# A diffusion-transformer layer on one core: four small moves of work between engines, steps and banks

## The chip, the core and the metric

The kernel runs on one NeuronCore of a Trainium2 chip. The metric is the time of one execution on the device in microseconds, and of several executions the median. A core has a matrix engine (TensorE, in the profile PE, its weight loads PEld), an engine for elementwise work and reductions (VectorE, DVE), one for activations (ScalarE, ACT), a general one (GpSimd, POOL) and one that issues DMAs (SyncE, SP). Each works through its own instructions strictly in program order and waits on semaphores for the others.

## What is computed

One layer of a transformer with two kinds of heads, over a sequence of 2048 rows of width 1024, beside a context of 256 rows:

```
h = modulate(rmsnorm(x), shift1, scale1);  hc likewise from the context
rq, rk, rv, rg, aq, ak, av = split(h @ w_in)      # context: rk, rv, ak, av only
ret = bidirectional chunked retention (4 heads of 128, chunk 128) on rope(rq), rope(rk), rv
ret = groupnorm(ret) * gn_g * silu(rg)
att = softmax attention, 8 query heads over 2 key heads of 64, keys = context + sequence
x   = x + g1 * (concat(ret, att) @ w_out)
h2  = modulate(rmsnorm(x), shift2, scale2)
x   = x + g2 * (relu(h2 @ w_ff1)**2 @ w_ff2)      # 1024 -> 4096 -> 1024
out = rmsnorm(x) * final_norm_g
```

Shifts, scales and gates come from a product of a conditioning vector with w_mod. All inputs are 32-bit floats; query and key heads are normalized ahead of the rotation (rope).

## The kernel before

Products are made of halves: an operand is split into a high half and a low remainder (16-bit, scaled by a power of two that depends on the operand's largest value), and three matmuls (high by high, high by low, low by high) add up in one PSUM bank. That is why maxima of the weights are needed: `greatest_of` loads a piece of a later weight (512 KB, L916) and VectorE takes its greatest magnitude into `wmx` (L919). 32 pieces are treated so.

**Input projection (to about 600 us).** The work of TensorE is a list of units, each one tile of 128 rows by one block of columns of w_in (24 matmuls, L1192 to L1194). The order of everything else is written out by hand: `do(s, part, fn)` files a piece of work under step s, and after each unit `run_step(s)` issues what is filed for that step, in the order of `PARTS`:

```
PARTS = ("hi", "evac", "turned", "low", "vec", "pool", "root", "aux", "turn", "load", "store")
```

"hi" holds the high halves of weights (ScalarE, L536) and keys, "evac" the copies of finished units out of PSUM (ScalarE, L699), "turned" the copies of turned retention heads (ScalarE, L740, tile zs), "low" the low halves (VectorE, L543), "vec" the rotation (VectorE, L635 to L650, which makes ys and kn), "aux" the maxima and rows of the modulation (VectorE, L919 and L380), "turn" the transposes by TensorE into one of two PSUM banks of the pool psT (tile psx: retention heads L711, attention keys L837), "load" and "store" the DMAs on SP's queue. Loads of w_in (L517, tile wst), of w_mod (L369, wmo) and of pieces for maxima (L916, wm) share one ring of six buffers under the tag "wst" (L301). A buffer goes to the next load in the order in which the loads are issued, and that load starts when the buffer's last user is done.

For an attention key tile whose unit is at step s (L815 to L842): split high at s+4 (ScalarE) and low at s+5 (VectorE, L832), `turn_k` at s+6 (TensorE, L837), and at s+7 the copy of the two turned blocks, 128 x 256, into `ks` (L842). Eighteen tiles have such a copy. For a retention query or key tile `turn` is at s+4 and `turned` at s+5.

**Attention, retention and output (to about 1460 us).** Here the order is a table of events: `on(k, phase, fn)`, with 36 events for each of the 16 tiles of rows, from the last tile (c = 15) to the first. A group of events holds score products (L210, L211, exponentials on ScalarE L216, high half L220, low half on GpSimd L227 or VectorE L229, products with values L242 to L245). A tile's retention output is copied out at event k+10, its statistics made at k+12 and k+13 (VectorE), the root and the row mr (GpSimd, L1689) in a chain behind, then four norms (ScalarE, L1695, one for each head) and the gating (GpSimd, L1699). The transposes of the gated rows (TensorE, L1815) follow at k+24 and the output product after that (L1833 to L1835). Tile t gets its residual sum (VectorE, L1840), norm (GpSimd, L1860), transposes (L1865), modulation (VectorE, L1870), shift (GpSimd, L1875) and the store of h2. For t = 0, the last, these four steps are not events but entries of the list `rest`, of which two are issued in each early step of the next stage.

**Feed-forward (from about 1462 us).** Up and down projections in seven Strassen products each. A job of the up-projection is 12 matmuls (L2071 to L2073) into one PSUM bank of the ring `ff["ps"]`; VectorE adds the result to its partners (L2083). The weights are summed by GpSimd, converted high by ScalarE (L2047) and low by VectorE (L2053). `Ring` (L1976) hands out slots in turn. It has four banks from the start, gets two more when `open_late` runs, and the last two when `rest` is empty (L2421 to L2425): these are the two banks that held the last tile's transposed rows. `extend` puts new slots ahead of the old ones, so that they are the next to be used; a tile in a bank starts when the bank's former reader is done.

Of the kernel before, what the change touches and what calls it, by code (L numbers as in the profile page):

```python
# [16 lines left out]
AF = mybir.ActivationFunctionType  # L17
ALU = mybir.AluOpType
AX = mybir.AxisListType
PSUM = bass.MemoryType.PSUM  # L20
DRAM = bass.MemoryType.DRAM

P = 128
# [33 lines left out]
def layer_kernel(ctx: ExitStack, tc: tile.TileContext, a: dict, out: bass.AP):  # L57
    nc = tc.nc
# [211 lines left out]
    with ExitStack() as st, tc.manual_schedule():  # L270
# [36 lines left out]
        def do(s, part, fn, *args):  # L307
            steps.setdefault((s, part), []).append((fn, args))
# [380 lines left out]
        def post(s, g, col, kind, i, x):  # L689
# [59 lines left out]
            elif col == C_RG:  # L749

                def gated():
                    nc.gpsimd.tensor_tensor(new_y(), x["x"], gnb, op=ALU.mult)

                def greatest():
                    nc.vector.tensor_reduce(
                        wmx[:, 72 + i : 73 + i], x["y"], axis=AX.X, op=ALU.max, apply_absolute_value=True
                    )

                do(s + 1, "evac", evac, AF.Silu)
                do(s + 2, "pool", gated)  # L760
                do(s + 3, "vec", greatest)
                do(s + 3, "store", lambda: nc.sync.dma_start(rg_d[i], x["y"]))
            elif col == C_AQ:
                att_tables(s, x, i)
                do(s + 1, "evac", evac)
                head_norm(s + 1, x, 8, "q", scale)
                rope(
                    s + 2,
                    x,
                    lambda: heads(new_y(), 8),  # L770
                    lambda: heads(x["x"], 8),
                    lambda: x["tb"][:, 0, 0],
                    lambda: x["tb"][:, 0, 1],
                    8,
                    HD,
                    lambda: bc(x["r"].unsqueeze(2), [P, 8, HD]),
                )
                do(s + 4, "turn", turn)

                def high():  # L780
                    x["z"] = op.tile([P, 2, 4, P], F16, name="qhl", tag="zs")
                    nc.scalar.activation(x["z"][:, 0], x["pt"], AF.Copy)

                def low():
                    nc.vector.tensor_tensor(x["z"][:, 1], x["pt"], x["z"][:, 0], op=ALU.subtract)

                do(s + 5, "turned", high)
                do(s + 5, "vec", low)
                do(s + 6, "store", lambda: nc.sync.dma_start(aq_d[i], x["z"]))
            else:  # L790
                do(s + 1, "evac", evac, AF.Copy, 256)
                src = lambda: x["x"][:, 128:256].rearrange("p (g d) -> p g d", g=2)
                do(s + 2, "store", lambda: nc.sync.dma_start(av_d[:, :, row], src()))
                head_norm(s + 1, x, 2, "k", scale)

                def new_k():
                    x["kn"] = op.tile([P, 2, 2, HD], F32, name="kn", tag="kn", bufs=4)
                    return x["kn"][:, :, 0]

                r = lambda: bc(x["r"].unsqueeze(2), [P, 2, HD])  # L800
                if kind == "c":

                    def plain():
                        w = bc(g2[:, 1, 0].unsqueeze(1), [P, 2, HD])
                        nc.gpsimd.tensor_tensor(new_k(), heads(x["x"][:, :128], 2), w, op=ALU.mult)

                    do(s + 2, "pool", plain)
                    do(
                        s + 3,
                        "vec",  # L810
                        lambda: nc.vector.tensor_tensor(x["kn"][:, :, 0], x["kn"][:, :, 0], r(), op=ALU.mult),
                    )
                else:
                    att_tables(s, x, i)
                    rope(  # L815
                        s + 2,
                        x,
                        new_k,
                        lambda: heads(x["x"][:, :128], 2),
                        lambda: x["tb"][:, 1, 0],  # L820
                        lambda: x["tb"][:, 1, 1],
                        2,
                        HD,
                        r,
                    )

                def high():
                    x["kh"] = op.tile([P, 2, HD], F16, name="kh", tag="kh")
                    nc.scalar.activation(x["kh"], x["kn"][:, :, 0], AF.Copy)

                def low():
                    nc.vector.tensor_tensor(x["kn"][:, :, 1], x["kn"][:, :, 0], x["kh"], op=ALU.subtract)  # L832

                def turn_k():
                    x["pt"] = psT.tile([P, 4, P], F32, name="psx", tag="psx")
                    for g in range(2):
                        nc.tensor.transpose(x["pt"][:, g], x["kn"][:, g].rearrange("p a b -> p (a b)"), ident)  # L837

                do(s + 4, "hi", high)
                do(s + 5, "low", low)  # L840
                do(s + 6, "turn", turn_k)
                do(s + 7, "vec", lambda: nc.vector.tensor_copy(ks[:, :, row * P : (row + 1) * P], x["pt"][:, :2]))  # L842

        def value_parts(s):

# [64 lines left out]
        def greatest_of(i, s):  # L910

            x = {}

            def load():
                x["w"] = raw("wm").rearrange("p a b -> p (a b)")
                nc.sync.dma_start(x["w"], piece_of(i))  # L916

            def reduce():
                nc.vector.tensor_reduce(wmx[:, i : i + 1], x["w"], axis=AX.X, op=ALU.max, apply_absolute_value=True)  # L919

            do(s - 1, "load", load)
            do(s, "aux", reduce)

        def magnitude_of(i, s):
# [609 lines left out]
    def on(k, phase, fn, *args):  # L1534
        events.setdefault((k, phase), []).append((fn, args))
# [74 lines left out]
    def retention(k0):  # L1610
# [110 lines left out]
        for n in range(NT):  # L1721
            c, k = NT - 1 - n, R0 + RF * n
            on(k - 8, "dma", take, c, "qt", "kt")
            on(k - 4, "late", decay, c, "qf", tf)
            on(k - 3, "late", decay, c, "qb", tb)
            on(k - 11, "dma", take, c + NC, *(("rk", "rv") if c > 0 else ("rv",)))
            on(k - 2, "dma", take, c, "f")
            on(k + 2, "pe", score, c, (0, 1, 2, 3))
            on(k + 4, "late", mask, c)
            for h in range(4):  # L1730
                on(k + 6 + h, "pe", head, c, h)
            if c > 0:
                on(k - 8 if n else k - 2, "late", weigh, 1, c + NC)
                on(k + 5, "pe", product, c + NC, 0, (0, 1, 2, 3))
                on(k + 8, "late", update, 1, c + NC, ("b", c), ("b", c - 1), "sb", (0, 1))
                on(k + 9, "late", update, 1, c + NC, ("b", c), ("b", c - 1), "sb", (2, 3))
            on(k + 10, "late", ocopy, c)
            on(k + 12, "dma", take, c, "gate")
            on(k + 12, "late", stats, c, (0, 1))
            on(k + 13, "late", stats, c, (2, 3))  # L1740
            on(k + 13, "late", root, c)
            for h in range(4):
                on(k + (16 + h // 2 * 2 if c > 0 else 15 + h // 2), "late", norm, c, h)
            on(k + (20 if c > 0 else 17), "late", gated, c)


    rest = []
# [56 lines left out]
    def output_tile(t, k, last):  # L1804
# [95 lines left out]
            return made  # L1900
        if t == 1:
            for q in range(2):
                on(k + 79 + q, "pe", transpose_x, q)
                on(k + 80 + q, "early", modulate, q)
                on(k + 81 + q, "late", shift_, q)
                on(k + 82 + q, "dma", store_h, q)
            return made
        on(k + 68, "pe", transpose_x, 0)
        on(k + 70, "early", modulate, 0)
# [66 lines left out]
    class Ring:  # L1976
# [4 lines left out]
            for slot in slots:  # L1981
                self.extend(*slot)

        def extend(self, pool, tag, n):
            at = self.n % max(len(self.slots), 1)
            self.slots = [(pool, tag, n)] * n + self.slots[at:] + self.slots[:at]
            self.n = 0

        def tile(self, shape, dtype, name):
# [418 lines left out]
    with tc.manual_schedule():  # L2408
        for k in range(min(events)[0], max(events)[0] + 1):
            for phase in PHASES:  # L2410
                run(k, phase)
                if phase in ("maximum", "low", "late"):
                    link()
        assert not events and not chain
        up_jobs()
        down_jobs()
        k = min(events)[0]
        while events:
            for phase in FPHASES:
                run(k, phase)  # L2420
                if phase == "pe" and rest and k > 1:  # L2421
                    rest_steps(2)
                    if not rest:
                        banks.close()
                        ff["ps"].extend(pool(late_ff, "fp3", space=PSUM), "p", 2)  # L2425
            k += 1


# [58 lines left out]
```

## Time and profile before

| | |
|---|---|
| time, median of 3 runs | 2643.18 us (2641.77 to 2645.54) |
| the profiled execution | 2639.86 us, of which the span is 2638.0 us |
| mean granted clock of TensorE | 0.997 |
| ScalarE, VectorE, GpSimd busy | 1504.4, 2045.0, 1761.0 us |
| moved by DMA | 481.84 MB, mean 183 GB/s |

The durations below are from the profiled execution. A row of the timeline gives the start in the span, the busy time, engine, line, operation, output and inputs with their shapes, and in brackets how long the engine had been idle before it and what ended that. The rows of waits sum such idle time by the instruction that waited and the one that released it. A row of windows gives, for a stretch of the span, the busy time of each engine with the number of its instructions, then TensorE's granted clock (1.00 is full speed), the mean busy share of the DMA engines, and GB/s.

### The profile page before, as it was taken

What the parts mean: (1) busy time and instruction counts of PE and PEld (TensorE: products, weight loads), DVE (VectorE), ACT (ScalarE), POOL (GpSimd) and SP (SyncE); (2) the same over time, 40 slices, a digit from 0 to 9 for tenths busy, and PEclk for the clock granted to TensorE, in tenths of its full rate; (3) what the DMA queues carried; (4) which work ended last, traced back from release to release, by engine and by line L of the source; (5) the groups of instructions that cost most, each with busy time, mean ns of one, the idle gap of its engine ahead of it and who ended that gap; (6) DMA issues with size and microseconds to landing.
All of it is one profiled execution on the core that took longest, in us unless ns stands there. A gap on an engine that the chain in (4) does not pass through costs nothing.

```text
span 2638.0 us, 45431 instructions
## 1 busy us (share of the span) xinstructions
PE 2595.5 (98%) x16617; PEld 1449.8 (55%) x16617; DVE 2045.0 (78%) x3098; ACT 1504.4 (57%) x2544; POOL 1761.0 (67%) x1451
## 2 busy tenths in 40 slices
PE   8999999999999999999999999999999999999998
PEld 5885555546666666666666444444444444444443
DVE  5788898667888888888887697899886665656686
ACT  3865343427877787888788576666665322222243
POOL 3644566546676678798887685777662566666686
PEclk9999999999999999999999999999999999999999
DMA  7776999737122132333332855777684748475453
GB/s 232 274 254 222 306 328 318 263 113 228 45 71 59 57 112 74 101 85 117 97 86 72 295 156 153 239 226 231 216 295 144 277 170 303 162 285 183 153 190 114
DMA packets 332903, 481.84 MB, mean 183 GB/s; under 512 B 90228, under 2 KB 200068, under 8 KB 328200
## 3 DMA queue, kind: packets, MB, share of 16 engines
q1 hardware_dynamic: 332664, 478.94, 54.9%
q8 instruction: 130, 2.13, 0.3%
q14 instruction: 93, 0.76, 0.1%
q10 hardware_dynamic: 16, 0.01, 0.0%
HBM read 321.89 MB, written 156.38 MB: 181 GB/s over the span
## 4 chain that ended last, share of the span: by engine, by line
PE 69%; ACT 3%; POOL 2%; DVE 1%; DMA 1%; issue 1%; DVEq 0%; POOLq 0%; ACTq 0%; SPq 0%
PE pd L2300 7%; PE pd L2298 7%; PE pd L2299 7%; PE pu L2071 7%; PE pu L2073 7%; PE pu L2072 7%; PE st L210 4%; PE o L245 4%; PE st L211 4%; PE mp L177 3%; PE o L243 2%; PE bank L1835 2%; PE bank L1833 2%; PE bank L1834 2%; ACT p L216 1%; ACT phi L220 1%
## 5 line engine op out<-in xcount | busy, mean ns | idle before, releaser
L190 DVE TENSOR_REDUCE nm<-mp 128x1 f32<-128x512 f32 x558 | 377.6, 685 | 88.3 <-PE mp L177 82.9
L216 ACT ACTIVATE p<-st 128x512 f32<-128x512 f32 x576 | 341.6, 600 | 153.7 <-PE st L211 148.0
L227 POOL TENSOR_TENSOR plo<-p,phi 128x1024 f16<-128x1024 f32 x160 | 348.8, 2186 | 83.2 <-ACT phi L220 83.1
L2071 PE MATMUL pu<-hf,w1f 128*128 128x512 f16 x896 | 339.6, 379 | 3.7 <-DVE u L1870 2.9
L2073 PE MATMUL pu<-hf,w1f 128*128 128x512 f16 x896 | 339.6, 379 | 0.4 <-DVE w1f L2053 0.4
L2298 PE MATMUL pd<-w,uf 128*128 128x512 f16 x896 | 339.6, 379 | 0.0
L2299 PE MATMUL pd<-w,uf 128*128 128x512 f16 x896 | 339.6, 379 | 0.0
L2300 PE MATMUL pd<-w,uf 128*128 128x512 f16 x896 | 339.6, 379 | 0.0
L2072 PE MATMUL pu<-hf,w1f 128*128 128x512 f16 x896 | 339.6, 379 | 0.0
L2318 POOL TENSOR_TENSOR y<-y,d 128x512 f32<-128x512 f32 x128 | 210.7, 1649 | 143.1 <-ACT uf L2287 98.6
L220 ACT ACTIVATE phi<-p 128x1024 f16<-128x1024 f32 x288 | 305.2, 1060 | 0.0
L229 DVE TENSOR_TENSOR plo<-p,phi 128x512 f16<-128x512 f32 x256 | 236.0, 923 | 21.8 <-ACT phi L220 9.4
L243 PE MATMUL o<-wv,plo 128*128 128x65 f16 x2304 | 230.1, 193 | 0.7 <-POOL plo L227 0.5
L245 PE MATMUL o<-wv,phi 128*128 128x129 f16 x2176 | 228.4, 220 | 0.0
L210 PE MATMUL st<-qr,ks 128*128 128x512 f16 x576 | 218.0, 379 | 10.3 <-ACT p L216 7.9
L243 PEld LDWEIGHTS <-plo 128*128 128x128 f16 x2304 | 205.1, 98 | 29.8 <-POOL plo L227 1.7
L2310 DVE SCALAR_TENSOR_TENSOR y<-pd,scy,y 128x512 f32<-128x512 f32 x160 | 116.9, 747 | 131.9 <-PE pd L2300 130.6
L211 PE MATMUL st<-qr,ks 128*128 128x512 f16 x576 | 218.2, 379 | 0.0
L2083 DVE TENSOR_TENSOR r<-pu,r 128x512 f32<-128x512 f32 x224 | 149.9, 684 | 83.9 <-PE pu L2073 59.9
L1192 PE MATMUL pso<-wf,h_l 128*128 128x512 f16 (+1 forms) x576 | 208.9, 363 | 0.0
L1193 PE MATMUL pso<-wf,h_l 128*128 128x512 f16 (+1 forms) x576 | 208.7, 362 | 0.0
L1194 PE MATMUL pso<-wf,h_l 128*128 128x512 f16 (+1 forms) x576 | 208.6, 362 | 0.0
(394 smaller groups left out, 6109.2 us busy)
## 6 DMA issues: line engine op xcount, KB each, us to landing
wm<-in_w_ff SPq DMA_DIRECT2D x64, 512.0 KB, 7.1
u<-r SPq DMA_DIRECT2D x128, 256.0 KB, 4.3
ur<-u SPq DMA_DIRECT2D x128, 256.0 KB, 5.9
y<-x SPq DMA_DIRECT2D x64, 512.0 KB, 6.3
wf<-w2f SPq DMA_DIRECT2D x112, 256.0 KB, 3.0
w<-wf SPq DMA_DIRECT2D x28, 1024.0 KB, 11.2
w1r<-in_w_ff SPq DMA_DIRECT2D x48, 512.0 KB, 5.2
x<-y SPq DMA_DIRECT2D x48, 512.0 KB, 2.6
```

What stands on the lines that cost most here:

```text
L190: nc.vector.tensor_reduce(dst, src, axis=AX.X, op=ALU.max, negate=True)
L216: nc.scalar.activation(self.p[kt // 2][:, kt % 2], self.s.pop(kt), AF.Exp, scale=HD**-0.5)
L220: nc.scalar.activation(hi, self.p[j], AF.Copy)
L227: nc.gpsimd.tensor_tensor(lo, p, hi, op=ALU.subtract)
L243: mm(o[:, : HD + 1], lo[:, i, c], v[:, : HD + 1], start=False, stop=False)
L245: mm(o, hi[:, i, c], v[:, :VW], start=False, stop=last)
L2071: mm(pu[hf, i], whi, hi, start=k == 0, stop=False)
L2072: mm(pu[hf, i], whi, lo, start=False, stop=False)
L2073: mm(pu[hf, i], wlo, hi, start=False, stop=k == 3)
L2298: mm(ps, u[:, 0, b], w[:, b, 0], start=b == 0, stop=False)
L2299: mm(ps, u[:, 0, b], w[:, b, 1], start=False, stop=False)
L2300: mm(ps, u[:, 1, b], w[:, b, 0], start=False, stop=b == 3)
```

## The change

Four things are moved; no arithmetic is added or left out.

1. The copy of turned keys goes from VectorE to ScalarE, and from part "vec" to part "turned" of the same step.
2. The load of a piece for maxima goes from part "load" to part "hi" of the same step, so it is issued ahead of that step's other loads.
3. The norms of the first tile of the attention (n = 0, c = 15) go from events k+16 and k+18 to k+18 and k+20, its gating from k+20 to k+22. In the second to last output tile (t = 1) transposes, modulation, shift and store go one event later each.
4. `Ring.extend` gets a flag with which new slots go behind the old ones, and the last two banks are added so.

```diff
                 do(s + 6, "turn", turn_k)
-                do(s + 7, "vec", lambda: nc.vector.tensor_copy(ks[:, :, row * P : (row + 1) * P], x["pt"][:, :2]))
+                ks_ = ks[:, :, row * P : (row + 1) * P]
+                do(s + 7, "turned", lambda: nc.scalar.activation(ks_, x["pt"][:, :2], AF.Copy))
...
-            do(s - 1, "load", load)
+            do(s - 1, "hi", load)
             do(s, "aux", reduce)
...
             for h in range(4):
-                on(k + (16 + h // 2 * 2 if c > 0 else 15 + h // 2), "late", norm, c, h)
-            on(k + (20 if c > 0 else 17), "late", gated, c)
+                on(k + (15 + h // 2 if c == 0 else (16 if n else 18) + h // 2 * 2), "late", norm, c, h)
+            on(k + (17 if c == 0 else 20 if n else 22), "late", gated, c)
...
         if t == 1:
             for q in range(2):
-                on(k + 79 + q, "pe", transpose_x, q)
-                on(k + 80 + q, "early", modulate, q)
-                on(k + 81 + q, "late", shift_, q)
-                on(k + 82 + q, "dma", store_h, q)
+                on(k + 80 + q, "pe", transpose_x, q)
+                on(k + 81 + q, "early", modulate, q)
+                on(k + 82 + q, "late", shift_, q)
+                on(k + 83 + q, "dma", store_h, q)
...
-        def extend(self, pool, tag, n):
+        def extend(self, pool, tag, n, last=False):
             at = self.n % max(len(self.slots), 1)
-            self.slots = [(pool, tag, n)] * n + self.slots[at:] + self.slots[:at]
+            new, old = [(pool, tag, n)] * n, self.slots[at:] + self.slots[:at]
+            self.slots = old + new if last else new + old
             self.n = 0
...
                         banks.close()
-                        ff["ps"].extend(pool(late_ff, "fp3", space=PSUM), "p", 2)
+                        ff["ps"].extend(pool(late_ff, "fp3", space=PSUM), "p", 2, True)
```

## The prediction

> **What bounds the kernel now.** The page's first lines come first: which engine has hardly any idle time.
>
> ```profile
> span 2638.0 us, 45431 instructions
> PE 2595.5 (98%) x16617; PEld 1449.8 (55%) x16617; DVE 2045.0 (78%) x3098; ACT 1504.4 (57%) x2544; POOL 1761.0 (67%) x1451
> ```
>
> TensorE works for 2595.5 of 2638.0 us. The change takes away none of its work, so all that can be won lies in 2638.0 − 2595.5 = 42.5 us of idle time, and in any time that its clock is lowered. The view of TensorE's waits says what ended that idle time (total us, times, longest):
>
> ```profile
> PE pu L2071 <- DVE u L1870: 2.9, 1, 2.9
> ...
> PE psx L837 <- DVE ks L842: 1.9, 1, 1.9
> ...
> PE psx L711 <- DVE ks L842: 1.7, 1, 1.7
> ```
>
> Each of the three is a single stall on a line that the change touches: two turns waiting for the copy of turned keys (L842), and one up-projection waiting for the last tile's modulation (L1870). Together 6.5 us; nothing else touched is longer than 0.6 us.
>
> **The change part by part.** *Keys copied by ScalarE, and maxima loaded earlier.* The timeline around the first stall:
>
> ```profile
> 363.76 1.22 DVE L919 TENSOR_REDUCE wmx<-wm 128x1 f32<-128x1024 f32 x1 [3.12 <-DMA wm<-in_w_ff]
> ...
> 367.43 0.42 DVE L842 CAST ks<-psx 128x256 f16<-128x256 f32 x1
> 367.90 0.61 PE L837 MATMUL psx<-ident,kn 128*128 128x128 f32 x2 [1.92 <-DVE ks L842]
> ```
>
> VectorE stood 3.12 us before L919 for a chunk, did what was queued behind, reached the copy at 367.43, and only then had TensorE a bank. The clock in the 4 us after the stall (columns: busy time with count of PE, PEld, DVE, ACT, POOL; granted clock; DMA share; GB/s):
>
> ```profile
> 368.00:372.00 4.00, 4.00 (x12) 1.66 (x13) 3.86 (x6) 1.49 (x3) 2.82 (x3) 0.57 1.03 386
> ```
>
> At a mean clock of 0.57, 4 us hold 2.3 us of full-speed work: 1.7 us are lost. So this place costs 1.92 + 1.7 = 3.6 us.
>
> The Trainium skill, "TensorE: Matmul & The Clock Gate", section "Part 1: The HAM clock gate (the "warmup" mystery)", has the clock halve after at least one idle window of about 3.4 us, in a window that runs free of the kernel. The trace doesn't bear out the first (a wait of 1.92 us was enough); by the second, the 1.7 us may fall in some executions and not in others, and by that the whole sum below would be 1.7 us smaller.
>
> The second stall:
>
> ```profile
> 413.87 0.69 ACT L699 ACTIVATE xs<-pso,sci 128x512 f32<-128x512 f32 x1 [3.06 <-PE pso L1194]
> ...
> 421.66 0.42 DVE L842 CAST ks<-psx 128x256 f16<-128x256 f32 x1
> 422.13 0.66 PE L711 MATMUL psx<-ident,ys 128*128 128x128 f32 x4 [1.72 <-DVE ks L842]
> ```
>
> "turned" stands right behind "evac" in the order of parts, so on ScalarE the copy would come behind the eviction that ends at 414.56, some 7 us before VectorE got to it. The 1.72 us go. What the copy costs ScalarE is bounded by two PSUM reads of its own:
>
> ```profile
> 359.68 0.58 ACT L740 ACTIVATE zs<-psx 128x512 f32<-128x512 f32 x1
> ...
> 361.20 0.46 ACT L699 ACTIVATE xs<-pso,sci 128x256 f32<-128x256 f32 x1
> ```
>
> I take 0.46 (same shape), against 0.58 as upper and 0.36 as lower end; 18 times 0.46 = 8.3 us on an engine that is 57% busy, and hidden. VectorE is relieved of 18 copies; it has the fuller queue in this stage:
>
> ```profile
> L842 DVE CAST ks<-psx x18: 409/411/425, 102.1 to 421.7; 128x256 f16<-128x256 f32 x18
> ```
>
> ```profile
> 304.00:360.00 56.00, 56.00 (x364) 35.79 (x362) 55.01 (x76) 25.01 (x45) 37.07 (x43) 1.00 0.90 309
> ```
>
> It is busy 55.01 of 56 us there, so each copy taken off lets all behind it come earlier. Six of them fall between these two:
>
> ```profile
> 308.50 0.41 DVE L842 CAST ks<-psx 128x256 f16<-128x256 f32 x1
> ...
> 350.77 0.41 DVE L842 CAST ks<-psx 128x256 f16<-128x256 f32 x1
> ```
>
> 6 × 0.41 = 2.5 us by 351, less what idle time VectorE had: I take 2.
>
> Moving the load has a price. The six raw buffers go to loads in the order in which these are issued, each when its last user is done with it, and "hi" is ahead of "load". Around the stall:
>
> ```profile
> 350.14 6.32 SPq L517 DMA_DIRECT2D wst<-in_w_in  x2
> ...
> 354.48 1.59 DVE L380 SCALAR_TENSOR_TENSOR macc<-wmo,cc,macc 128x512 f32<-128x512 f32 x2
> ...
> 355.87 2.19 ACT L536 ACTIVATE wf<-wst,sci 128x1024 f16<-128x1024 f32 x2 [3.01 <-DMA wst<-in_w_in]
> ...
> 357.54 0.38 SPq L916 DMA_DIRECT2D wm<-in_w_ff  x1
> ...
> 362.77 0.60 PE L711 MATMUL psx<-ident,ys 128*128 128x128 f32 x4
> ```
>
> ```profile
> DMA to landing us min/median/max: 5.3/6.5/8.6
> ```
>
> Now a weight chunk starts at 350.14 and lands at 355.87 (5.73 us); the chunk for the maxima starts last, at 357.54, and lands at 363.76. In the new order the maxima take the buffer that came free at 350.14, and the weight chunk waits for the next, freed by L380 at 354.48 + 1.59 = 356.07 (or by 354.1 with VectorE 2 us ahead). VectorE's 3.12 us are gone, but the weight lands at about 354.1 + 5.7 = 359.8 to 356.1 + 5.7 = 361.8, up to 6 us later than 355.87. ScalarE works in order: from this weight's start (355.87) to the end of zs (359.68 + 0.58 = 360.26), which frees a turn bank, it took 4.39 us. TensorE wants the bank at 362.77. A slip of 3.9 to 5.9 us gives zs at 364.2 to 366.2, a new stall of 1.4 to 3.4 us; if the weight finds a buffer still 2 us sooner, none. I take 1 us, nearer to none, because VectorE, relieved, may free the buffer sooner, and ScalarE idled 3.01 us before that weight, which leaves the work ahead of it done. So of 3.6 us at this place 2.6 are won: 1.92 + 1.7 − 1.0. What is late next is VectorE's low half of the weight, ahead of ys:
>
> ```profile
> 373.90 0.68 DVE L648 TENSOR_TENSOR ys<-t,t 128x512 f32<-128x512 f32 x1
> ...
> 375.04 0.60 PE L711 MATMUL psx<-ident,ys 128*128 128x128 f32 x4
> ```
>
> VectorE reaches ys earlier by the 3.12 us and the copies, later by the weight's slip of 4 to 6 us: a turn at 371.5 to 378 in place of 375.04, which takes from the 2.6 us or adds nothing: TensorE cannot be ahead of its ys. I charge 0.6 for it: **2.0** here, **1.7** at 422, between ends of −1 and 5.3 together. The other 31 chunks I price at nothing: no wait of TensorE on them is in the view of waits, and they only change places with loads whose users start microseconds later.
>
> *Last banks at the end of the ring.* The timeline (the 0.60 at 1490.34 is an older wait, which stays):
>
> ```profile
> 1489.61 1.28 DVE L2083 TENSOR_TENSOR r<-pu,r 128x512 f32<-128x512 f32 x2
> 1490.34 0.38 PE L2071 MATMUL pu<-hf,w1f 128*128 128x512 f16 x1 [0.60 <-DVE r L2083]
> 1491.77 1.28 DVE L2083 TENSOR_TENSOR r<-pu,r 128x512 f32<-128x512 f32 x2
> ...
> 1495.28 1.27 DVE L1870 TENSOR_TENSOR u<-bank,a 128x512 f32<-128x512 f32 x2
> 1496.01 0.38 PE L2071 MATMUL pu<-hf,w1f 128*128 128x512 f16 x1 [2.92 <-DVE u L1870]
> ```
>
> The job at 1496.01 takes a bank that the last tile's modulation still held; under the new order its bank is one whose product VectorE added at 1489.61 to 1490.89, free for 2 us before 1496.01 − 2.92 = 1493.09. A job takes 1493.09 − 1490.34 = 2.75 us. The two late banks come up when the older six have gone round, so even two jobs later, at 1498.6, L1870 is past (1495.28 + 1.27 = 1496.55). So **2.9** go, unless L2083's later adds are late: the next pair ends by 1491.77 + 1.28 = 1493.05, for jobs further on. Ends: 0 and 2.92.
>
> *First tile's norms two steps later.*
>
> ```profile
> 651.11 0.88 ACT L1695 ACTIVATE oo<-oo,mr,cy_gn 128x128 f32<-128x128 f32 x2 [1.15 <-POOL mr L1689]
> ...
> 652.52 0.38 PE L210 MATMUL st<-qr,ks 128*128 128x512 f16 x1 [0.57 <-ACT p L216]
> ...
> 653.95 0.38 PE L210 MATMUL st<-qr,ks 128*128 128x512 f16 x1 [0.57 <-ACT p L216]
> ...
> 655.58 1.27 POOL L1699 TENSOR_TENSOR oo<-oo,ogate 128x512 f32<-128x512 f32 x1
> ...
> 656.63 0.38 PE L210 MATMUL st<-qr,ks 128*128 128x512 f16 x1 [0.53 <-ACT p L216]
> ...
> 658.09 2.50 POOL L227 TENSOR_TENSOR plo<-p,phi 128x1024 f16<-128x1024 f32 x1 [1.24 <-ACT phi L220]
> ...
> 660.81 0.60 PE L1815 MATMUL bank<-ident,oo 128*128 128x128 f32 x4
> ```
>
> ScalarE stands 1.15 us for mr ahead of the norms, and three score products then wait 0.57 + 0.57 + 0.53 = 1.67 us on its exponentials. Two steps later mr is long there, so that 1.15 goes; but two pairs of 0.88 us still stand before exponentials, and gated, on GpSimd behind plo (658.09 + 2.50 = 660.59), ends at 660.59 + 1.27 = 661.86, 1.05 us past the transposes' 660.81. 1.67 − 0.4 (still late) − 1.05 = **+0.2**; ends −1.5 and +1.2.
>
> *Second tile's steps one event later.*
>
> ```profile
> 1465.86 0.66 PE L1865 MATMUL bank<-ident,xr 128*128 128x128 f32 x4 [0.53 <-DVE xr L1840]
> ...
> 1487.40 0.39 PE L2073 MATMUL pu<-hf,w1f 128*128 128x512 f16 x1 [0.41 <-DVE w1f L2053]
> ```
>
> The 0.53 us go, but TensorE then comes 0.5 us sooner to weights for whose conversion it waits 0.41 now: given back. **0**, ends −0.5 and +0.5.
>
> **Sum:** 2.0 + 1.7 + 2.9 + 0.2 + 0 = 6.8 us. The profiled execution has 2638.0 us of span (2639.86 in all), 3.3 us under the median 2643.18 of the runs; taken off the median, 2643.18 − 6.8 = **2636.4**. One measurement of this kernel tells about 0.2% (5.3 us) from no change: faster begins below 2637.9, slower above 2648.5.
>
> **The rivals.**
> *The whole place is won*: the weight's chunk finds its buffer soon enough that nothing waits at 362.77 and the clock stays up: 3.6 + 0.4 of ready work + 1.7 + 2.9 + 1 = 9.6, giving 2633.6, down to 2631. For it: VectorE is the full engine and is relieved. Against: L380's 356.07. Chance 0.12.
> *The stall only moves*: the wait at L919 becomes a wait for the weight behind it; TensorE stands about 3.4 us at 362.77, clock loss included or not: the first place nets 0 to −1, so −1 + 1.7 + 2.9 to 1.7 + 2.9 = 3.6 to 4.6, and up to 5: 2638 to 2641.5. For it: ScalarE's in-order 4.39 us. Chance 0.24.
> *The change doesn't do what it says*: the bank that is next is again late and each key copy waits on ScalarE's queue instead: 2641.5 to 2645. Against: evictions end 7 us before. Chance 0.07.
> *Slower*: the same mechanism, larger. If the weight takes the longest landing seen, 8.6 us, from the second issue (350.14 + 6.32 = 356.46), it is there at 365.1, zs ends at 369.5, TensorE stands 6.7 us, and with 1.7 of clock 8.4, against 3.6 + 1.7 + 2.9 + 0.2 = 8.4 won: exactly even. It decides from there: each further microsecond, or a second chunk held like this one, is a loss; one more at 1.4 to 6.7 gives 2645 to 2650. For it: DMA share of 1.03 in the window. Against: one weight in 32 would have to be the latest. Chance 0.05, most of it above 2648.5.
>
> **How the numbers follow.** Forecast 2633 to 2639 with 0.52, of it 0.07 above 2637.9; whole place 0.12; moved 0.24; nothing 0.07; slower 0.05. Faster: 0.45 + 0.12 = 0.57; slower 0.04; the rest, 0.39, within 0.2%. The range 2631.5 to 2642 leaves out most of the last two cases and a little of the whole win, some 0.13.
>
> **What would show it.** Right: no DVE wait at the L919 near 363; ks on ScalarE ending within 2 us of each eviction; no wait of TensorE at the places of 367.90, 422.13 and 1496.01; clock 1.00 after 368. Wrong: a ScalarE wait for wst above 5 us near 356 with a PE wait on zs (L740) behind it; a wait for an L2083 add in the ring; the transposes L1815 waiting for oo. If a long PE wait stands at another place in the first 600 us, my price of nothing for the other 31 chunks was the error.

## The result, and the profile after

| | median | runs | ratio to the kernel before (95%) |
|---|---|---|---|
| before | 2643.24 us | 22 | |
| changed | 2638.05 us (2634.19 to 2641.46) | 22 | 0.998 (0.9973 to 0.9986) |

The change wins 5.2 us (3.7 to 7.1, from the interval times 2643.24); 6.8 were forecast. The page of the changed kernel's profiled execution (2635.67 us) begins:

```profile
span 2633.9 us, 45447 instructions
PE 2594.3 (98%) x16617; PEld 1450.6 (55%) x16617; DVE 2043.7 (78%) x3080; ACT 1509.5 (57%) x2562; POOL 1762.5 (67%) x1451
```

The 18 copies show in the counts (DVE 3098 to 3080, ACT 2544 to 2562). A copy took 0.38 us on ScalarE (median) where it had taken 0.41 on VectorE; 18 × 0.41 = 7.4 us left VectorE, but its busy time fell by 1.3 only, so its other instructions took some 6 us more in all. Some of them are shown below. What changed stands in the view of TensorE's waits:

```profile
PE mp L177 <- DVE nm L190: 2.5, 3, 1.9
...
PE psx L711 <- DVE ys L648: 2.1, 1, 2.1
PE bank L1634 <- DMA orv<-rv: 1.9, 3, 1.3
PE bank L1816 <- POOL oo L1700: 1.2, 1, 1.2
...
PE psx L711 <- ACT zs L740: 0.9, 1, 0.9
PE pu L2073 <- ACT w1f L2049: 0.9, 1, 0.9
```

The three waits that headed the list (u 2.9, ks 1.9, ks 1.7) are gone. In their stead stand two of the same kind, for ys and zs, one for the gating, one for a weight, and a larger sum at nm and orv. Line numbers are one or two higher than before in the later parts of the kernel.

Both traces hold 16617 matmuls in the same order, but for 12 near 1465 us, where the second tile's transposes change places with the matmuls beside them (in e5, e7 and e9, below, 6 near 661 us do so too). So the start of the same matmul in the two traces, one minus the other, says how far TensorE is ahead, and the change of that difference over a stretch says what the stretch won (negative) or lost. The same is done below for every kernel against the first profile of before:

| us | 360–380 | 380–430 | 600–645 | 645–665 | 1490 to end |
|---|---|---|---|---|---|
| changed | −0.3 | −2.6 | +2.0 | +0.1 | −3.1 |
| changed, again (e11) | −0.3 | −2.6 | +4.5 | +0.1 | −3.1 |
| before, again (e10) | −0.6 | −0.2 | +0.9 | 0.0 | +1.5 |
| e1 keys copied by ScalarE, alone | −1.0 | −2.6 | −0.1 | 0.0 | +1.2 |
| e2 load ahead, alone | +0.3 | 0.0 | +1.2 | 0.0 | +0.2 |
| e3 ring, alone | −0.6 | 0.0 | +3.1 | 0.0 | −3.1 |
| e4 all but the load | +1.0 | −2.7 | +4.6 | +0.1 | −3.1 |
| e5 norms and transposes | −0.5 | +0.2 | −0.4 | −0.5 | +2.5 |
| e6 gate product later | −2.4 | +1.5 | −0.3 | +0.1 | −3.1 |
| e7 three mended | −2.1 | +1.5 | +3.6 | −0.5 | −3.1 |
| e8 two maxima moved, alone | −2.4 | −2.2 | −0.1 | 0.0 | +2.0 |
| e9 change, two maxima moved | −2.7 | −2.7 | +3.6 | −0.5 | −3.1 |
| e12 all but the ring | −0.2 | −2.7 | +2.2 | +0.1 | −1.2 |

The stretches left out scatter by 1.6 us at most.

How 360 to 380 went in the changed kernel, in the timeline:

```profile
349.83 0.35 SPq L917 DMA_DIRECT2D wm<-in_w_ff  x1
355.77 1.56 SPq L517 DMA_DIRECT2D wst<-in_w_in  x2
...
359.49 2.19 ACT L536 ACTIVATE wf<-wst,sci 128x1024 f16<-128x1024 f32 x2 [8.22 <-DMA wst<-in_w_in]
360.67 1.28 DVE L543 SCALAR_TENSOR_TENSOR wf<-wst,sci,wf 128x1024 f16<-128x1024 f32 x1 [2.53 <-ACT wf L536]
363.30 0.58 ACT L740 ACTIVATE zs<-psx 128x512 f32<-128x512 f32 x1
363.93 0.66 PE L711 MATMUL psx<-ident,ys 128*128 128x128 f32 x4 [0.93 <-ACT zs L740]
...
369.24 3.56 DVE L380 SCALAR_TENSOR_TENSOR macc<-wmo,cc,macc 128x512 f32<-128x512 f32 x2
369.87 2.38 POOL L1041 TENSOR_TENSOR wor<-wor,early 128x1024 f32<-128x1024 f32 x1 [0.38 <-DMA wor<-in_w_out]
373.92 0.68 DVE L648 TENSOR_TENSOR ys<-t,t 128x512 f32<-128x512 f32 x1
374.74 0.63 PE L711 MATMUL psx<-ident,ys 128*128 128x128 f32 x4 [2.14 <-DVE ys L648]
```

The chunk for maxima took the first place in the queue (349.83), the weight followed at 355.77 and was there at 359.49, 3.6 us later than before. ScalarE stood 8.22 us for it, zs ended at 363.88, TensorE waited 0.93. VectorE no longer waited 3.12 us at the maximum but 2.53 for the weight's high half: 0.6 us won, and 0.3 more as the copy was gone. But three instructions behind the maximum took longer than before. First two of them in the changed kernel, then the same two before:

```profile
363.99 1.59 DVE L543 SCALAR_TENSOR_TENSOR wf<-wst,sci,wf 128x1024 f16<-128x1024 f32 x1
...
366.24 1.74 DVE L1049 TENSOR_TENSOR wof<-wor,wof 128x1024 f16<-128x1024 f32 x1
```

```profile
364.90 1.28 DVE L543 SCALAR_TENSOR_TENSOR wf<-wst,sci,wf 128x1024 f16<-128x1024 f32 x1
...
366.30 1.22 DVE L1048 TENSOR_TENSOR wof<-wor,wof 128x1024 f16<-128x1024 f32 x1
```

With L832 between them (0.81 in place of 0.28) that is 1.4 us more. GpSimd's rotation runs beside them: it waits for VectorE's hs_k, which now comes behind the late weight, and started at 362.84 instead of 360.54. The same three times stand in e11 and e2 below, which have the load ahead too, and not in e1 and e4, which have it in its old place. GpSimd's product of 2.38 us cost no more than before: now two L380 took 3.56 us beside it where two took 1.59, and before it was an L543 that took 3.38 where one takes 1.28. In all, ys started at 373.92; before it was at 373.90. VectorE reached this point at the same time, TensorE came earlier, and the wait is the difference. The wait at the place of 367.90 and the lowered clock behind it are gone:

```profile
368.00:372.00 4.00, 4.00 (x20) 1.77 (x19) 3.86 (x5) 1.48 (x3) 3.27 (x3) 1.00 1.00 364
```

The turns that waited at 414.57 and 422.13 come without a wait, those of the first tile's gated rows with a new one, and the job of 1496.01 without:

```profile
413.81 0.49 PE L711 MATMUL psx<-ident,ys 128*128 128x128 f32 x3
419.31 0.60 PE L711 MATMUL psx<-ident,ys 128*128 128x128 f32 x4
```

```profile
658.04 1.72 POOL L1700 TENSOR_TENSOR oo<-oo,ogate 128x512 f32<-128x512 f32 x1
659.81 0.66 PE L1816 MATMUL bank<-ident,oo 128*128 128x128 f32 x4 [1.24 <-POOL oo L1700]
```

```profile
1491.87 0.38 PE L2073 MATMUL pu<-hf,w1f 128*128 128x512 f16 x1
1492.87 1.27 DVE L1871 TENSOR_TENSOR u<-bank,a 128x512 f32<-128x512 f32 x2
```

1496.01 became 1491.87, before the modulation (1492.87) that it had to wait for.

### The profile page after: what moved, and what is told of

It reads as the page before. It is cut to its first block, busy times and chain, and to the rows that moved or that the text cites. A ratio compares the mean times of both kernels' runs of the same rounds, so it can differ in the third digit from the quotient of the medians.

```text
span 2633.9 us, 45447 instructions
## 1 busy us (share of the span) xinstructions
PE 2594.3 (98%) x16617; PEld 1450.6 (55%) x16617; DVE 2043.7 (78%) x3080; ACT 1509.5 (57%) x2562; POOL 1762.5 (67%) x1451
## 4 chain that ended last, share of the span: by engine, by line
PE 84%; DVE 5%; ACT 4%; DMA 3%; POOL 2%; issue 2%; SPq 0%; DVEq 0%; POOLq 0%; ACTq 0%
PE pd L2302 7%; PE pd L2300 7%; PE pd L2301 7%; PE pu L2073 7%; PE pu L2075 7%; PE pu L2074 7%; PE pso L1193 4%; PE pso L1195 4%; PE pso L1194 4%; PE st L210 4%; PE o L245 4%; PE st L211 4%; PE mp L177 3%; PE o L243 2%; PE bank L1836 2%; PE bank L1834 2%
## 5 line engine op out<-in xcount | busy, mean ns | idle before, releaser
L227 POOL TENSOR_TENSOR plo<-p,phi 128x1024 f16<-128x1024 f32 x160 | 347.0, 2174 | 86.2 <-ACT phi L220 86.1
L229 DVE TENSOR_TENSOR plo<-p,phi 128x512 f16<-128x512 f32 x256 | 236.3, 924 | 21.2 <-ACT phi L220 8.7
```

Source lines behind the costliest of these rows:

```text
L227: nc.gpsimd.tensor_tensor(lo, p, hi, op=ALU.subtract)
```

## The experiments

**Theory** after the traces: edit 1 removes the stalls at 414 and 422 by itself; at 368 it would remove the wait for ks too, but TensorE then waits for ys, since VectorE is the bound of that stretch; edit 2 trades a wait for the chunk against a wait for the weight and is worth nothing. **Rival**: the load is what frees the first place.

### e1: keys copied by ScalarE, alone

```diff
-                do(s + 7, "vec", lambda: nc.vector.tensor_copy(ks[:, :, row * P : (row + 1) * P], x["pt"][:, :2]))
+                ks_ = ks[:, :, row * P : (row + 1) * P]
+                do(s + 7, "turned", lambda: nc.scalar.activation(ks_, x["pt"][:, :2], AF.Copy))
```

> The kernel before with edit 1 alone (turned keys copied by ScalarE). Theory: the stalls at 414.57 and 422.13 go by this edit alone (-2.6 us), since ScalarE is idle there. At 367.90 the wait for ks goes too, but VectorE still stands 3.1 us at L919 for the chunk, reaches ys of the next turn no earlier, and TensorE waits there instead (1.5 to 3 us for ys): net 0 to -1.5 us with the clock. In all -2.6 to -4 us. Rival (the load is what frees the first place): the stall at 367.90 stays or grows, only -2.6 us or less in all, and the whole gain of the change at 360 to 380 needs edit 2.

Measured: 2640.37 us, ratio 0.9991 (0.9982 to 1.0). VectorE's timeline:

```profile
362.69 1.22 DVE L920 TENSOR_REDUCE wmx<-wm 128x1 f32<-128x1024 f32 x1 [2.47 <-DMA wm<-in_w_ff]
...
369.80 3.37 DVE L543 SCALAR_TENSOR_TENSOR wf<-wst,sci,wf 128x1024 f16<-128x1024 f32 x1
373.10 0.68 DVE L648 TENSOR_TENSOR ys<-t,t 128x512 f32<-128x512 f32 x1
```

and TensorE's waits from 340 to 440, one row:

```profile
PE psx L711 <- ACT sq L659: 2.6, 1, 2.6
```

The wait at 368 and those at 414 and 422 are gone by this edit alone, though VectorE still stood 2.47 us for the chunk. The row names sq, which ended within 0.03 us of ys; the turn came 0.14 us after the end of ys, as in the changed kernel, so I read it as the wait for ys. The theory holds: −1.0 and −2.6. Against the second profile of before (e10), where the clock stayed up at this place as it did here, the first is −0.4.

### e2: load ahead, alone

```diff
-            do(s - 1, "load", load)
+            do(s - 1, "hi", load)
```

> The kernel before with edit 2 alone (chunks for maxima issued ahead of the other loads). Theory: VectorE's 3.1 us at L919 go, but the weight chunk behind lands about 3.6 us later, ScalarE waits 8 us for it instead of 3 and VectorE 2.5 us for its high half; zs makes TensorE wait about 1 us near 363, and the wait for ks near 367.9 stays at 1 to 2 us as VectorE gets to the copy no sooner; the stalls at 414.57 and 422.13 stay. Within 1 us of the kernel before, rather slower (+0 to +1.5 us). Rival: the wait at L919 was the cause, and without it the first place is won: -2 to -3.6 us.

Measured: 2641.8 us, ratio 1.0001 (0.9992 to 1.001). Waits of ScalarE, VectorE and TensorE at this place:

```profile
ACT wf L536 <- DMA wst<-in_w_in: 8.6, 1, 8.6
```

```profile
DVE wf L543 <- ACT wf L536: 2.4, 1, 2.4
```

```profile
PE psx L711 <- DVE ks L842: 1.7, 1, 1.7
PE psx L711 <- ACT zs L740: 1.2, 1, 1.2
PE psx L837 <- DVE ks L842: 1.2, 1, 1.2
PE psx L711 <- DVE ys L648: 1.1, 1, 1.1
```

At this place TensorE had one wait in the first profile of before (1.9 us, and the lowered clock) and two in the second (1.6 and 1.2); here it has three (1.2 + 1.2 + 1.1 = 3.5 us). The rival fell: without the wait for the chunk nothing is won, and against the second profile 0.9 us are lost.

### e3: the ring, alone

```diff
-            self.slots = [(pool, tag, n)] * n + self.slots[at:] + self.slots[:at]
+            new, old = [(pool, tag, n)] * n, self.slots[at:] + self.slots[:at]
+            self.slots = old + new if last else new + old
```

> The kernel before with the ring's edit alone (last two banks behind the old ones). Theory: the wait of 2.9 us for the last tile's modulation goes and nothing takes its place: -2.9 us, all of it at 1496. Rival: a job a little later waits for an add (L2083) or a weight (L2053) instead, and 1 us or more of it is given back by 1520.

Measured: 2636.75 us, ratio 0.9981 (0.9972 to 0.999). TensorE's waits from 1480 to 1530:

```profile
PE pu L2072 <- DVE r L2084: 0.6, 1, 0.6
PE pu L2074 <- DVE w1f L2054: 0.4, 1, 0.4
PE pu L2072 <- ACT w1f L2048: 0.2, 1, 0.2
```

The 2.9 us are gone, the three smaller waits are those that were there, and nothing came later: −3.1. The time fell by 5 us (2.6 to 7.4), more than the wait; what can add to it is the clock, below. By time alone this one edit can't be told from the whole change (5.2 us, 3.7 to 7.1): the parts have to be read by their places in the table.

### e4: all but the load

> The changed kernel with edit 2 undone (load back in its old place), edits 1, 3, 4 and the ring kept. Theory: edit 2 trades VectorE's wait for the chunk against a wait for the weight; without it the place at 360 to 380 nets the same within 0.7 us, so the time is that of the changed kernel within 1 us. Rival: edit 2 is worth what was forecast for that place, 2 us: then this kernel is 2 us slower than the changed one and TensorE waits 2 us more between 360 and 380.

The edit is that of e2, backwards; the expectation counts the two halves of edit 3 as edits 3 and 4. Measured: 2636.39 us, ratio 0.9981 (0.9972 to 0.9989). The median is 1.7 us under the changed kernel's, the ratio to the kernel before is the same (0.998). VectorE stood 3.3 us for the chunk again and TensorE waited 2.5 us at ys and 0.4 at kn. In this execution the clock fell behind that wait (0.62 from 376 to 380), which makes the table's +1.0 out of some −0.7 (an estimate: 1.7 us of clock taken off). The changed kernel has −0.3 there, so edit 2 wins nothing and seems to cost 0.4 us (0.7 if e1 is compared with the changed kernel).

### e5: norms two steps later, transposes one

```diff
-            on(k + at[0], "pe", transpose, w)
+            on(k + at[0] + (t == NT - 1 and w == "r"), "pe", transpose, w)
```

with the norms' part of edit 3, on the kernel before.

> The kernel before with the first tile's norms and gating two steps later (edit 3, first half), and the transposes of that tile's gated rows one event later too (k+25). Theory: in the changed kernel the norms win 1.4 us between 651 and 658 and lose it at 660, where the transposes wait 1.2 us for the gating behind GpSimd's plo. With the transposes one event later the loss goes: progress of TensorE -1.2 to -1.5 us from 650 to 665, none given back. Rival: what the transposes feed (the split at k+26, the products at k+28) is late next, and 1 us or more is given back by 675.

One execution, 2642.35 us. The norms won 1.4 us and 0.9 were given back, 0.6 of it by the transposes, which still wait for the gating: net −0.5, where −1.2 to −1.5 were expected. The place is right and the size was less than half.

### e6: the gate product one step later

```diff
-                b = s + 3 + 3 * k
+                b = s + 3 + 3 * k + (k == 6)
```

on the changed kernel.

> The changed kernel with the seventh piece of output weights (load, gate product on GpSimd, split, store) one step later. Theory: what gave the gain at 360 to 380 back is VectorE, whose L380 took 2.73 us instead of 0.75 while GpSimd's 2.38 us gate product ran beside it, ahead of ys. Without that product there ys ends 2 us sooner, the wait of 2.14 us at 374.74 falls to 0.3 us or less, and TensorE is 2 us further at 380. Later it may cost 0 to 2 us again, as the product then slows VectorE at 380 to 390. Rival: ys is held by the late weight (VectorE's wait of 2.5 us for its high half), or by the sum of VectorE's work, and L380 is slow for another reason: the wait stays at 1.5 us or more.

Measured: 2637.78 us, ratio 0.9988 (0.998 to 0.9997): not faster than the changed kernel. Timeline of VectorE, GpSimd and TensorE:

```profile
370.51 1.59 DVE L380 SCALAR_TENSOR_TENSOR macc<-wmo,cc,macc 128x512 f32<-128x512 f32 x2
...
374.04 0.63 PE L711 MATMUL psx<-ident,ys 128*128 128x128 f32 x4 [0.16 <-DVE ys L648]
...
376.54 2.40 POOL L1041 TENSOR_TENSOR wor<-wor,early 128x1024 f32<-128x1024 f32 x1
376.83 2.25 DVE L650 TENSOR_TENSOR kn<-kn,ry_k 128x128 f32<-128x128 f32 x1
...
415.37 0.79 PE L711 MATMUL psx<-ident,ys 128*128 128x128 f32 x4 [2.10 <-DVE qhl L785]
```

```profile
416.00:420.00 4.00, 4.00 (x13) 1.53 (x12) 3.90 (x8) 1.64 (x3) 3.92 (x4) 0.60 1.06 393
```

The step was right: without GpSimd's product beside it the pair of L380 takes 1.59 us again, and the wait for ys fell from 2.14 to 0.16. But the product went where it stopped another instruction (L650, 2.25 us for one that takes 0.29 alone), and TensorE, 2 us further, caught VectorE up at 415 instead: 2.10 us of wait and a lowered clock. Won and lost again; the bound is VectorE's whole queue up to 420, not one place in it. From 374 to 416 VectorE was idle for 0.9 us in all (0.7 in the changed kernel).

### e7: three places mended

On the changed kernel: the load back in its old place, `do(s + (i == 12), "aux", reduce)` for the maximum that was waited for, e6's step and e5's transposes.

> The changed kernel with three more moves: the load for maxima back in its old place and instead the one maximum that VectorE waited 3.1 us for taken one step later; the gate product of e6 one step later; the first tile's transposes one event later as in e5. Theory: the three places net -0.9 and -2.1 us (360 to 380) and -1.2 us (660): 2 to 4 us under the changed kernel, 2634 to 2636. Rival: the buffer held a step longer makes a weight or a row of w_mod late in turn, TensorE waits between 365 and 400, and the time is that of the changed kernel or above.

Measured: 2638.15 us, ratio 0.9986 (0.9977 to 0.9995): the changed kernel's time. TensorE waited 1.5 us for ys and 2.1 us for qhl at 416. The expectation failed, for e6's reason: what is only shifted within the stretch stays in VectorE's queue.

### e8 and e9: two maxima out of the stretch

```diff
-        at = [39, 40, 41] + list(range(43, 64, 2)) + list(range(66, 84))
+        at = [39, 40, 41] + list(range(43, 60, 2)) + sorted([*range(66, 84), 78, 81])
```

e8 is this alone on the kernel before. e9 is the changed kernel with it, the load in its old place, and e5's transposes.

> The kernel before, with none of the change's edits; only the two pieces whose maxima are taken at steps 61 and 63 go to steps 78 and 81. Theory: TensorE's stalls between 360 and 425 are set by VectorE's total work there, 63 of 66 us; two maxima (2.4 us) and the wait of 3.1 us before one of them leave it, so the copy of keys, ys and qhl all come 2 to 5 us sooner: the waits of 1.9, 0.6 and 1.7 us go, with the clock loss where there was one, and nothing comes instead: -3.5 to -6 us, the gain that was forecast for edits 1 and 2 together. Rival: the end in that stretch is set by loads (weights, rows of w_mod) and by GpSimd's gate product beside VectorE: a wait for ys of 1 us or more stays at 375, and half of the gain or less is seen.

> The changed kernel with the load for maxima in its old place, the two maxima of e8 moved, and the first tile's transposes one event later (e5). Theory: all waits between 360 and 425 go (-3 us against the changed kernel: 0.9 and 2.1), 0.6 us are won at 660: 2634 to 2636, the fastest kernel of the study. Rival: moved pieces crowd the loads of steps 77 to 81 and give 1 us or more back near 470.

Measured: e8 2638.92 us, ratio 0.999 (0.9981 to 0.9999); e9 2634.22 us, ratio 0.997 (0.9959 to 0.9982). TensorE's waits from 340 to 440, e8 and then e9:

```profile
PE psx L711 <- ACT sq L659: 1.2, 1, 1.2
PE psx L711 <- DVE qhl L785: 0.3, 1, 0.3
```

```profile
PE psx L711 <- ACT sq L659: 0.9, 1, 0.9
```

Two maxima less there, and none of the change's edits, win 2.4 + 2.2 us in the stretch: more than edits 1 and 2 together won. The time shows less (2.9 us, 0.3 to 5.0), as the wait at 1496 stayed in e8 and was longer (3.2) with the clock lowered behind it. e9 is the lowest time of the study; its interval overlaps that of the changed kernel. About 1 us of the wait for ys is left in both (the rows name sq, which ended within 0.03 us of ys), as e8's rival had it; that half of the gain or less would be seen, as it also said, did not come.

### e10, e11, e12: the same kernels again, and all but the ring

> The kernel before, unchanged, for a second profile of it. Theory: what differs between profiles of one kernel is the halved clock behind a wait of TensorE of 1.5 us or more (1.7 us, in some executions) and a place in the retention at 616 to 640 us, where loads of rv land in a different order against the rest (0 to 4 us); the waits of 1.7 to 2.9 us at 368, 422 and 1496 stay within 0.5 us. Rival: these waits themselves vary by 1 us or more from one execution to the next, and a comparison of two profiles tells nothing of them.

> The changed kernel, unchanged, for a second profile. Theory: the waits of 0.9 us for zs near 364, 2.1 us for ys near 374 and 1.2 us for the gating near 660 come again within 0.5 us, the ring's wait is gone again; the place at 616 to 640 and the clock may differ. Rival: the wait for ys is 1 us or less in this execution, and what was found at 374 was chance.

> The changed kernel with the ring's edit undone. Theory: the wait for the last tile's modulation is back, 2.6 to 3.7 us, and the clock behind it halves in some executions: 3 to 5 us slower than the changed kernel, 2641 to 2643. Rival: TensorE comes later or earlier to this place by the other edits, so that the wait is under 2 us and the time within 2 us of the changed kernel's.

e10 (one execution, 2642.20 us) and e11 (one, 2639.81 us) bear the theory out: before waited 1.6, 1.7 and 2.7 us at the three places, the changed kernel 1.0, 2.2 and 1.2 us at zs, ys and the gating. What differed was the clock (full behind 368 in e10, halved behind its wait at 1496) and the stretch from 600 to 645.

In e12 (2638.28 us, ratio 0.9989, 0.998 to 0.9998) the rival was right on the size of the wait; the median lies 0.2 us from the changed kernel's, the ratios 2.4 us apart:

```profile
PE pu L2072 <- DVE u L1871: 1.7, 1, 1.7
PE pu L2072 <- ACT w1f L2048: 1.0, 1, 1.0
```

The wait is shorter because the modulation started 1.96 us sooner than before (1493.32), while TensorE came to the held bank 0.74 us sooner. Between VectorE's adds and the modulation stand two low halves of weights (L2053, here L2054). Beside GpSimd's sums of weights (L2042) they took 1.03 + 1.79 us before, here 0.73 + 0.86; the second of them before, and then here:

```profile
1492.96 1.79 DVE L2053 SCALAR_TENSOR_TENSOR w1f<-w1s,sc,w1f 128x512 f16<-128x512 f32 x1
```

```profile
1491.93 0.86 DVE L2054 SCALAR_TENSOR_TENSOR w1f<-w1s,sc,w1f 128x512 f16<-128x512 f32 x1
```

That is 1.23 us less, and the wait is 1.23 us shorter (2.92 to 1.69). In each of the seven profiles that have this wait (1.7 to 3.7 us) it is the sum of these two durations and 0.1 us. So in these profiles the ring's edit was worth 3.1 alone and 1.9 (3.1 − 1.2) on top of the others; whether the other edits make the two low halves shorter, or chance does, isn't shown. The wait of 1.0 us for a weight (0.2 before) goes with the second tile's later steps: all seven profiles that have them show 0.9 to 1.3 us there, all others 0.3 at most.

## Why the prediction was right, and where not

The time lies in the range and on the right side, 1.65 us above the forecast. By its steps:

- **367.90, priced at 2.0: this failed.** The table has 0.3 won against the first profile of before and 0.3 lost against the second. The first half went as worked out: the weight at 359.49 (359.8 to 361.8 said), a wait of 0.93 for zs (1.0 taken). The failed step is behind it: 1.92 and 1.7 were booked as won in full, with 0.6 charged for ys, and the wait for ys was 2.14. By the prediction's own rows ys ended at 373.90 + 0.68 = 374.58 and the turn came at 375.04. In the changed kernel the turn came 0.14 us after ys, so with ys at the same time no more than 0.3 us was to be won here. The prediction let VectorE come to ys earlier by the 3.12 us and the copies; it came at the same time, because 2.53 us of waiting moved with the weight and three instructions beside GpSimd took 1.4 us more. The rival "the stall only moves" had the place's number right, 0 to −1, but put the stand of 3.4 us at 362.77; 0.93 fell there and 2.14 at ys.
- **The 1.7 us of clock** are not a price of the place: in e3, e5 and e10, which have its wait of 1.5 to 1.7 us, the clock stayed up. Behind this wait it fell in the first profile of before alone, on which the sum was built. Nor were 1.7 us to be won: with the clock up, TensorE waited 1.2 to 1.3 us for ys in these three, and the stretch from 360 to 380 was only 0.5 to 0.6 us shorter. In the first profile the lowered clock hid that wait. That the 1.7 us may fall in some executions and not in others, as the prediction says, was borne out.
- **422.13, priced at 1.7: 2.6 measured**, in the changed kernel and in e1. The 0.57 at 414.57 went too; it is one of the waits of up to 0.6 us that the prediction left out of its sum. The copy took 0.38 us on ScalarE (0.46 taken), and is hidden, as was said.
- **The ring, 2.9: 3.1 measured.** Right, alone.
- **Norms, +0.2 won: 0.1 lost.** The mechanism was as told: 1.43 us won by 658, and the transposes wait 1.24 us (1.05 forecast).
- **Second tile, 0: 0.** 0.6 won at 1465 and 0.7 lost near 1486, where TensorE waits 0.88 us for a weight's high half from ScalarE (0.22 before). The prediction put this at VectorE's low half, whose 0.41 stayed as it was.
- **Price of nothing for the other 31 chunks.** It holds: from 80 to 600 us no wait of TensorE of 0.4 us or more was ended by a load, in any profile.

Summed: 0.3 + 2.6 + 3.1 − 0.1 = 5.9 by places, against 5.2 by time and 4.1 by the two profiled spans (2638.0 − 2633.9). The difference to the spans is the stretch from 600 to 645 (+2.0). That the total came within 1.65 us of the forecast is partly luck: 1.7 too much at the first place stands against 0.9 and 0.2 too little at 422 and in the ring, and single profiles differ by more than that through the clock and that stretch, for which the sum has no term (the span of e11 is 4.1 us longer than that of the changed kernel's first profile).

**That stretch, and what stays open.** Against the first profile of before, seven lose 2.0 to 4.6 us there (both of the changed kernel, e3, e4, e7, e9, e12) and six 1.2 at most. These seven are the profiles in which TensorE waits 1.84 to 1.89 us for a maximum (nm) that VectorE is late with. In the changed kernel:

```profile
630.06 2.09 DVE L229 TENSOR_TENSOR plo<-p,phi 128x512 f16<-128x512 f32 x1
...
633.17 0.38 PE L177 MATMUL mp<-ks,qr 128*128 128x512 f16 x1 [1.89 <-DVE nm L190]
```

and the first row's counterpart before, with no such wait behind it:

```profile
631.63 1.58 DVE L229 TENSOR_TENSOR plo<-p,phi 128x512 f16<-128x512 f32 x1
```

In these seven VectorE's last two low halves (L229) ahead of that maximum took 3.6 to 4.0 us together and GpSimd's low halves (L227) beside them 2.1 each; in the other seven profiles it was 2.2 to 2.6 us, and 2.6 for each of GpSimd's. So the two engines stand in each other's way, and which of them stands decides the stretch. The four with the largest losses (3.6 to 4.6) also have half clock behind the wait. What decides which engine stands is open: in e3 every engine has the same operations in the same order as before up to there, so the edits can't do it by their order; whether it is chance, or something that goes with the program, these runs don't tell.

## What to carry to other kernels

Where an engine is busy 55 of 56 us, as VectorE is here, a stall that it causes is a symptom of its queue: taking away one wait brought it to the next one at the same time, and only work taken out of the stretch (key copies, two maxima) moved the end. Ask of a load that is moved ahead which load now comes second; here it cost at least what it won. A bank that joins a ring while its last reader is late belongs at the end of the ring. And before a stall is booked as won, look when the waiting engine's next input comes: here the next wait took most of it back.

## What the runs showed of the hardware

**Behind a wait the clock halves in some executions and not in others.** In the fourteen profiles (before, changed, e1 to e12), TensorE waited 1.5 us or more 31 times between 300 and 1600 us; behind 12 of these waits the granted clock halved, behind none of the 43 waits of 1.0 to 1.5 us did it. The shortest wait with it was 1.84 us, the longest without it 2.92 and 3.12: none of the 10 waits from 1.5 to 1.8 us was followed by it, 12 of the 21 longer ones were. The same wait of 1.89 us for nm was followed by it in e11 and not in the first profile of the changed kernel. A window behind the wait of 2.62 us at 1492.34 in e1:

```profile
1492.00:1496.00 4.00, 3.66 (x11) 1.38 (x11) 4.00 (x6) 4.00 (x8) 3.63 (x3) 0.59 0.56 176
```

A mean of 0.59 over 4 us is half speed for 8 × 0.41 = 3.3 us; the row of before (0.57) gives 3.4. So a wait of more than 1.8 us costs itself and, in about half of the cases, up to 1.7 us more: an estimate from these counts, and less where a later wait hides it, as the one for ys did at 375. The Trainium skill ("TensorE: Matmul & The Clock Gate", section "Part 1: The HAM clock gate (the "warmup" mystery)") has a free-running window of about 3.4 us; the length and the chance agree with that, while its condition of an idle window of that length does not: 1.84 us were enough.

**VectorE and GpSimd stop each other.** L380 took 2.73 us in place of 0.75 (3.56 and 1.59 for the pair) beside a GpSimd product of 2.38, L650 2.25 in place of 0.29 beside one of 2.40; each ended 0.1 to 0.6 us after GpSimd's. Near 630 us it was at times GpSimd that took longer (2.6 in place of 2.1) and at times VectorE. The Trainium skill ("SBUF — State Buffer", section "Who interferes with whom") says that an instruction of VectorE with two inputs in SBUF contends with one of GpSimd that reads SBUF, and (section "SBUF: two separate sides") that whichever starts first has the shared port for the whole instruction; these rows agree. In a profile such a row shows as a long instruction, not as a wait. The stretch near 630 and the wait at 1496 vary from profile to profile in this way.
